# First rounds' modulation as a TensorE product in four column groups, with four load buffers

## The chip, the cores and the metric

One core of a Trainium2 chip runs the program. It has a matrix engine (TensorE), a vector engine (VectorE), an engine for activations and copies (ScalarE), GpSimd, and a queue engine (SyncE, SP in the profile) that issues most loads. The metric is the device time of one execution in microseconds; lower is better.

## The reference

One block of a hybrid network on `x` (256 tokens, 2048 wide), in float32. A conditioning vector `c` gives six modulation vectors of 2048 each, the first two of which scale and shift the normed input before the wide projection `w_in`; everything after needs that projection.

```python
mod = silu(c) @ w_ada + b_ada                       # 2048 -> 6 * 2048
sh1, sc1, gt1, sh2, sc2, gt2 = split(mod, 6)
h = rms_norm(x, norm1_g) * (1.0 + sc1) + sh1
proj = h @ w_in                                     # 2048 -> 10064
o_a = rwkv7_mix(proj[:rwkv])                        # recurrent half
o_b = nsa_mix(proj[rwkv:rwkv + nsa])                # attention half
x = x + gt1 * ((sig(m1) * (o_a @ w_o_rwkv) + sig(m2) * (o_b @ w_o_nsa)) @ w_out)
h = rms_norm(x, norm2_g) * (1.0 + sc2) + sh2
x = x + gt2 * (square(relu(h @ w_up)) @ w_down)
```

## The kernel before

All activations lie transposed: `xn[:, j]` holds rows 128 j to 128 j + 127 of the normed input's 2048 features, 256 tokens wide. Matrix products are done in three passes of a shorter float format: an operand is split into a high part (`hi`, a cast on ScalarE) and a low part (`lo = raw - hi`, on VectorE), and `mm3` (L101) adds hi*hi, lo*hi and hi*lo.

**Modulation.** `mod` is 96 columns of 128 values, kept in `modc[:, e]`. Column e is a dot product of a 128x2048 block of the transposed `w_ada` with `silu(c)` spread over all partitions (`sb`): `ada_long(e)` (L165) loads one megabyte into `ap` and lets VectorE multiply and sum it in one instruction (`ada_dot`, L156). Shift columns are 0 to 15, scale columns 16 to 31. `apb` has room for four blocks; the first four loads use all four, later ones only two (`SLOTS = 2`), so the third load from there on waits until the first one's dot is done.

**Rounds.** The projection's first nine column groups need all 2048 features, but start before all of `mod` is there: `rounds = [(0, 2), (2, 2), (4, 4), (8, 4), (12, 4)]` (L182) names the feature columns j of each round and their number. Each round first turns its columns into `am = (1 + sc) * norm1_g` and `hhi`, `hlo` (`modulate`, L326), and then runs nine groups of columns over its k rows, two at a time. One such **step** is a load `wr` of two k rows x 512 columns (352 in the first group, in three DMAs), the cast `whi`, the low part `wlo`, and 24 (18) matmuls of 256 tokens. Round 0 and round 1 have 9 steps each, round 2 and round 3 have 18 each: steps 1 to 9, 10 to 18, 19 to 36 and 37 to 54. After round 0 (which ScalarE copies) the sums of a group in PSUM (`pp`) are added to SBUF on VectorE, two banks a group (`acc_evac`); two groups, `pvp`, stay in PSUM through all rounds. `whi` and `wlo` have three buffers each, `wr` has four.

`next_ada` (L236) is called once a step and puts the loads and dots of the next round's columns among the steps: four columns for each two k rows.

**What sets the order.** The tile framework orders the instructions of each engine when the program is built, by priorities (`prio(STREAM)` comes before the main work) and its own notion of time. On the chip each engine then works through its list in order; a load waits in SP's list until its buffer is free. The names in the rows are those of the code: `ap` blocks of `w_ada`, `wr` blocks of `w_in`, `hf` an intermediate of `modulate`, `prk`, `pq`, `pl` the sums in SBUF, `pss` the sum of squares for the norm, `cps` the spread of `c`. Rows with a number behind the name tell buffers of one name apart.

Of the kernel before, what the change touches and what calls it, by code (L numbers as in the profile page):

```python
# [25 lines left out]
P_BADA, P_N1, P_N2, P_MU, P_A0, P_KK, P_KA, P_RK, P_LNW, P_LNB = 0, 96, 112, 128, 155, 163, 171, 179, 187, 195  # L26
P_QG, P_KG0, P_KG1, P_KG2, P_PEK, P_PEV, NPRM = 203, 204, 205, 206, 207, 223, 239

# [4 lines left out]
def block_kernel(ctx, tc, a):  # L33
# [128 lines left out]
    apn = [0]  # L162
    SLOTS = 2

    def ada_long(e):  # L165

        n = apn[0] if apn[0] < 4 else apn[0] % SLOTS
        r = apb[n // 2][:, n % 2]
        apn[0] += 1
        nc.sync.dma_start(r, a["w_ada_t"][e * 128:(e + 1) * 128])  # L170
        ada_dot(r, sb, prm[:, P_BADA + e:P_BADA + e + 1], modc[:, e:e + 1])
# [10 lines left out]
    rounds = [(0, 2), (2, 2), (4, 4), (8, 4), (12, 4)]  # L182
    for j in range(rounds[0][1]):
        ada_long(j)
        ada_long(16 + j)

# [56 lines left out]
    def proj(segs_of, W, ms, rhi, rlo, kps, evac, banks=None, first=True, last=True):  # L243
# [4 lines left out]
        for i, kp in enumerate(kps):  # L248
            hi, lo = weights(segs_of(kp), W)
            next_ada(ada_long if starting[0] else ada)  # L250
            todo = [[(k, m) for m in range(len(ms))] for k in range(2)]
# [39 lines left out]
    for k in range(2):  # L291
        mm(pss, ones, sqs[:, k], k == 0, k == 1)

# [7 lines left out]
    def rsqrt(out, x, scale, ep, tmp):  # L301

        e0 = {0.0: 0, 1e-6: 1, 64e-5: 2}[ep]
        act(out, x, AF.Ln, scale=scale, bias=eps[0:x.shape[0], e0:e0 + 1])
        i = act(out, out, AF.Exp, scale=-0.5)
        tt(tmp, out, out, OP.mult)
        stt(tmp, x, ep / scale, tmp, OP.add, OP.mult)
        stt(tmp, tmp, -0.5 * scale, out, OP.mult, OP.mult)
        stt(out, out, 1.5, tmp, OP.mult, OP.add)
        return i  # L310

    rs = T2("rs", [128, T])
    with tc.issue_after(log_exp([lastt])):
        rsqrt(rs, pss, 1.0 / D, 1e-6, T2("rst", [128, T]))

# [34 lines left out]
    pl = cst.tile([128, 3, T], FT, name="pl")  # L350
    pvp = [PX("pvp") for _ in range(4)]
    M4 = [(i * 128, 128) for i in range(4)]
# [19 lines left out]
    for i in range(2):  # L372
        groups.append(([(2048 + i * 512, 512)], 512, M4, None, pvp[2 * i:2 * i + 2]))
    for i in range(2):
# [9 lines left out]
    for r, (j0, n) in enumerate(rounds):  # L384
        first, last = r == 0, r == len(rounds) - 1
        with prio(START + (1 << 18)):
            stt(am[:, j0:j0 + n], modc[:, 16 + j0:16 + j0 + n], 1.0, prm[:, P_N1 + j0:P_N1 + j0 + n], OP.add, OP.mult)
            lasth = modulate(j0, n, xn)
            if first:
                hold.extend([lasth] * 0 + [None])  # L390
        if not last:
            later.extend(e for j in range(j0 + n, sum(rounds[r + 1])) for e in (j, 16 + j))
            pace[:] = [len(later) / (len(groups) * n // 2 - 1), 0]
        for cols, W, ms, dst, banks in groups:
            g = proj(wseg(cols), W, ms, hhi, hlo, range(j0 // 2, (j0 + n) // 2),
# [739 lines left out]
    with tc.issue_after(le):  # L1135
        i = rsqrt(rs2, ps[:, 0:T], 1.0 / D, 1e-6, T2("rst2", [128, T]))
    ahold[:0] = [i, i]
# [115 lines left out]
def _pack(inp):  # L1253
# [21 lines left out]
    out = {  # L1275
        "xT": g["x"].T, "c": g["c"], "w_ada_t": g["w_ada"].T, "w_in": g["w_in"], "params": p, "consts": c,
        "onehot": onehot, "w2a": np.concatenate([g["rwkv_w2"], g["rwkv_w0"][None]]), "a2": g["rwkv_a2"],
# [22 lines left out]
```

## Time and profile before

| | |
|---|---|
| median of three runs | 1647.45 us (1645.04 to 1648.28) |
| profiled execution | 1648.3 us, of which the span is 1646.5 us |
| TensorE (PE) busy | 1564.2 us, 95% |
| VectorE (DVE) busy | 1149.4 us, 70% |
| ScalarE (ACT) busy | 756.3 us, 46% |
| DMA, mean | 232 GB/s over the span, 371 GB/s in its first fortieth |

The span is what the trace shows between the first and the last instruction. Shares over the whole span hide the stretch that the change is about, the first 206 us; the tables by stage and the engines' timelines of that stretch are what to read.

### The profile page before, as it was taken

Reading aid. Unit: us, or ns where it says so; the run is one execution under the profiler, and the core shown is the slowest. Engines: PE = TensorE matmul, PEld = TensorE weight load, DVE = VectorE, ACT = ScalarE, POOL = GpSimd, SP = SyncE. Lnnn points to the kernel's source line nnn. Section 1 sums busy time; section 2 is a strip of 40 time slices with the busy share of each in tenths; the row PEclk is TensorE's granted clock in tenths of the full one; section 3 lists DMA queues with packets and bytes.
Section 4 is the critical chain, followed back from the end, with each engine's and each line's share of the span. In section 5 each row is a group of like instructions: output and inputs, shape, how many; then the busy total and the mean of one; then the engine's idle time right before and its main releaser. Section 6 shows DMA issues by size and latency. Waiting matters only on the chain.

```text
span 1646.5 us, 28130 instructions
## 1 busy us (share of the span) xinstructions
PE 1564.2 (95%) x11291; PEld 1380.2 (84%) x11291; DVE 1149.4 (70%) x1695; ACT 756.3 (46%) x1112; POOL 34.9 (2%) x60
## 2 busy tenths in 40 slices
PE   5969999999999889999999899999999999999998
PEld 4968998878889879777899788888888888888886
DVE  7999876977788766777876776666655555555555
ACT  4423358526423365656534444444444544444442
POOL 0000000000000000000000000000000000000001
PEclk9989999998999999999999999999999999999999
DMA  9999767673988777655687477878776555555564
GB/s 371 319 325 342 247 183 236 215 200 120 324 245 276 251 262 258 237 180 167 212 287 269 153 242 239 264 244 260 242 217 189 204 194 193 192 192 194 194 194 148
DMA packets 171174, 381.99 MB, mean 232 GB/s; under 512 B 29249, under 2 KB 43905, under 8 KB 166690
## 3 DMA queue, kind: packets, MB, share of 16 engines
q1 hardware_dynamic: 149344, 355.79, 65.6%
q0 software_dynamic: 4176, 14.17, 2.4%
q10 hardware_dynamic: 17523, 10.24, 2.2%
q8 instruction: 88, 1.44, 0.3%
q14 instruction: 43, 0.35, 0.1%
HBM read 370.13 MB, written 10.01 MB: 231 GB/s over the span
## 4 chain that ended last, share of the span: by engine, by line
PE 48%; DMA 4%; DVE 3%; issue 1%; ACT 1%; DVEq 0%; ACTq 0%
PE pu L99 21%; PE da L99 10%; PE db L99 10%; PE pp L99 5%; DMA ar<-in_w_ada_t 2%; DMA wr<-in_w_out 1%; DVE wlo L90 1%; PE po L99 1%; PE sps L99 1%; DMA gate<-sma 0%; ACT whi L193 0%; PE ptp L1012 0%; DVE ar L158 0%; DVE o L90 0%; ACT p L87 0%
## 5 line engine op out<-in xcount | busy, mean ns | idle before, releaser
L193 ACT CAST whi<-wr 128x1024 fp32r<-128x1024 f32 (+1 forms) x352 | 367.0, 1043 | 513.4 <-PE pp L99 125.6
L90 DVE TENSOR_TENSOR wlo<-wr,whi 128x1024 fp32r<-128x1024 f32 (+1 forms) x352 | 425.8, 1213 | 171.8 <-ACT whi L193 168.7
L99 PE MATMUL pp<-hhi,whi 128*128 128x256 f32 (+1 forms) x1072 | 309.9, 293 | 25.1 <-ACT hhi L87 22.5
L99 PE MATMUL pp<-hlo,whi 128*128 128x256 f32 (+1 forms) x1072 | 307.4, 289 | 0.2 <-DVE hlo L93 0.2
L99 PE MATMUL pp<-hhi,wlo 128*128 128x256 f32 (+1 forms) x1072 | 301.2, 290 | 6.6 <-DVE wlo L90 6.6
L90 DVE TENSOR_TENSOR wdl<-wd,wdh 128x1024 fp32r<-128x1024 f32 x128 | 156.6, 1225 | 170.9 <-ACT wdh L193 170.9
L99 PEld LDWEIGHTS pp<-hhi,whi 128*128 128x128 f32 (+1 forms) x1072 | 209.9, 197 | 33.8 <-ACT hhi L87 23.4
L193 ACT CAST wdh<-wd 128x1024 fp32r<-128x1024 f32 x128 | 134.9, 1055 | 193.7 <-PE db L99 188.6
L99 PEld LDWEIGHTS pp<-hhi,wlo 128*128 128x128 f32 (+1 forms) x1072 | 205.5, 196 | 13.0 <-DVE wlo L90 8.5
L99 PEld LDWEIGHTS pp<-hlo,whi 128*128 128x128 f32 (+1 forms) x1072 | 210.5, 196 | 5.0 <-issue 3.7
L99 PE MATMUL pu<-h2a,whi 128*128 128x512 f32 x512 | 177.2, 398 | 3.1 <-DVE h2a L93 3.1
L99 PE MATMUL pu<-h2b,whi 128*128 128x512 f32 x512 | 179.1, 397 | 0.8 <-DVE h2b L93 0.8
L99 PE MATMUL pu<-h2b,wlo 128*128 128x256 f32 x512 | 140.9, 280 | 0.0
L99 PE MATMUL pu<-h2a,wlo 128*128 128x256 f32 x512 | 135.9, 281 | 0.0
L158 DVE CUSTOM_DVE_ANT_0 ar<-ar,sb,prm 128x1024 f32<-128x1024 f32 x64 | 82.1, 1282 | 73.0 <-DMA ar<-in_w_ada_t 72.9
L99 PEld LDWEIGHTS pu<-h2b,whi 128*128 128x128 f32 x512 | 95.8, 188 | 23.9 <-DVE h2b L93 1.2
L99 PEld LDWEIGHTS pu<-h2a,whi 128*128 128x128 f32 x512 | 95.2, 189 | 24.4 <-DVE h2a L93 3.4
L99 PEld LDWEIGHTS pu<-h2a,wlo 128*128 128x128 f32 x512 | 95.5, 190 | 2.2
L158 DVE CUSTOM_DVE_ANT_0 ar<-ar,sb,adap 128x1024 f32<-128x1024 f32 x64 | 82.0, 1281 | 21.2 <-DMA ar<-in_w_ada_t 20.9
L99 PEld LDWEIGHTS pu<-h2b,wlo 128*128 128x128 f32 x512 | 95.9, 189 | 0.5
L99 PE MATMUL db<-wdh,ul 128*128 128x512 f32 x256 | 79.6, 389 | 0.0
L99 PE MATMUL db<-wdl,uh 128*128 128x512 f32 x256 | 79.6, 389 | 0.0
(342 smaller groups left out, 2676.6 us busy)
## 6 DMA issues: line engine op xcount, KB each, us to landing
wr<-in_w_in SPq DMA_DIRECT2D x136, 512.0 KB, 5.1
ar<-in_w_ada_t SPq DMA_DIRECT2D x128, 512.0 KB, 4.8
wr<-in_w_up SPq DMA_DIRECT2D x128, 512.0 KB, 4.3
wd<-in_w_down SPq DMA_DIRECT2D x128, 512.0 KB, 4.3
ap<-in_w_ada_t SPq DMA_DIRECT2D x32, 1024.0 KB, 6.6
wr<-in_w_out SPq DMA_DIRECT2D x32, 512.0 KB, 5.4
wr<-in_w_in SPq DMA_DIRECT2D x40, 256.0 KB, 3.4
wr<-in_w_o_rwkv SPq DMA_DIRECT2D x16, 512.0 KB, 4.9
```

The lines of the kernel that those rows point to most:

```text
L90: return V.tensor_tensor(out, x, y, op=op).ins
L99: return PE.matmul(out, l, r, start=start, stop=stop, skip_group_check=True).ins
L158: V.tensor_tensor_reduce(out=r, in0=r, in1=s, scale=0.5, scalar=start, op0=OP.mult, op1=OP.add, accum_out=out)
L193: S.copy(hi, raw)
```

## The change

- The columns of rounds 0 and 1 (0 to 3 and 16 to 19) are no longer dots on VectorE. `ada_pair((j, q))` handles two shift and two scale columns in four quarters q: it loads one megabyte of `w_ada_p` (a copy of `w_ada` rearranged on the host: per partition four blocks of 512 values, 256 shift and 256 scale columns each) and issues four float32 matmuls with 32 columns of weights each, `scz[:, 4q + i]` (2 silu(c) in column 0, zeros beside it), on the four column groups of the array, into the 32 rows of `adp` that belong to each. After the fourth quarter the bank is copied to `row`, and four matmuls against a column of ones add the four groups and turn the result, into `adc`; two additions put it into `modc`.
- Round 0's four quarters are issued at the start, the last two behind the norm's sum of squares; round 1's four are put into round 0.
- `later` of round 0 holds these four quarters and columns 4, 20 and 5 of round 2 (as dots); round 1 gets the other five. So round 2's eight columns are split three and five where round 1 had all eight.
- `ada_long` rotates through four buffers at all times.
- In round 0 the two `pvp` groups come last, and their four banks are allocated then.
- Two constraints (`ahold`, `hold`) put the first casts behind the norm's exponential and the first low parts behind the norm and `hlo`.

```diff
-    SLOTS = 2
...
-        n = apn[0] if apn[0] < 4 else apn[0] % SLOTS
+        n = apn[0] % 4
...
-    for j in range(rounds[0][1]):
-        ada_long(j)
-        ada_long(16 + j)
+    scz = T2("scz", [128, 16, 32])
+    V.memset(scz, 0.0)
+    sct = T2("sct", [128, 16])
+    act(sct, prm[:, P_C:P_C + 16], AF.Tanh, scale=0.5)
+    stt(scz[:, :, 0], sct, 1.0, prm[:, P_C:P_C + 16], OP.add, OP.mult)
+    adp = [None]
+
+    def ada_pair(x, after=None, copy_after=None):
+        j, q = x
+        n = apn[0] % 4
+        r = apb[n // 2][:, n % 2]
+        apn[0] += 1
+        nc.sync.dma_start(r, a["w_ada_p"][j * 256 + q * 128:j * 256 + q * 128 + 128])
+        if q == 0:
+            adp[0] = PX("adp")
+        with tc.issue_after(after) if after else contextlib.nullcontext():
+            for i in range(4):
+                mm(adp[0][32 * i:32 * i + 32], scz[:, 4 * q + i], r[:, i * 512:i * 512 + 512], q == 0, q == 3)
+        if q == 3:
+            row, ps = T2("adr", [128, 512]), PX("adc")
+            with tc.issue_after(copy_after) if copy_after else contextlib.nullcontext():
+                S.copy(row, adp[0])
+            for i in range(4):
+                mm(ps[:, i:i + 1], row[:, i * 128:i * 128 + 128], one, i == 0, i == 3)
+            for i, e in enumerate((j, 16 + j)):
+                stt(modc[:, e:e + 2], ps[:, 2 * i:2 * i + 2], 0.5, prm[:, P_BADA + e:P_BADA + e + 2], OP.mult, OP.add)
+
+    for q in range(2):
+        ada_pair((0, q))
...
+    ahold.extend([firsts[0]] * 3)
+    for q in range(2, 4):
+        ada_pair((0, q), i, firsts[0])
...
-                hold.extend([lasth] * 0 + [None])
+                hold.extend([lasth, lasth, firsts[1]])
...
+        if first:
+            later[:] = [(2, q) for q in range(4)] + [4, 20, 5]
+            pace[:] = [0.9, 0]
+        elif r == 1:
+            later[:] = [e for e in later if e not in (4, 20, 5)]
+            pace[:] = [len(later) / 8, 0]
+
-        for cols, W, ms, dst, banks in groups:
+        for cols, W, ms, dst, banks in sorted(groups, key=lambda g: g[3] is None) if first else groups:
+            if banks is not None:
+                if first:
+                    pvp.extend(PX("pvp") for _ in range(2))
+                banks = pvp[2 * banks:2 * banks + 2]
```

What the framework makes of it shows in three places. On TensorE, from the last spread of `c` to the first projection matmul, before:

```order
L99 MATMUL cps_123<-crow_94,one1_96 128x512
L99 MATMUL cps_127<-crow_94,one1_96 128x512
L99 MATMUL cps_131<-crow_94,one1_96 128x512
L99 MATMUL pss_149<-sqs_150,cs_103 128x256 x2
L99 MATMUL pp_202<-hhi_184,whi_208 128x256
```

and after:

```order
L99 MATMUL cps_131<-crow_94,one1_96 128x512
L99 MATMUL adp_143<-ap0_135,scz_137 32x512 x4
L319 MATMUL pss_157<-sqs_158,cs_103 128x256 x2
L99 MATMUL adp_143<-ap0_135,scz_137 32x512 x4
L99 MATMUL adp_143<-ap1_136,scz_137 32x512 x8
L99 MATMUL adc_203<-cs_103,adr_202 128x1 x4
L99 MATMUL pp_225<-hhi_211,whi_231 128x256
```

The sixteen small matmuls of round 0's columns stand around `pss`, and the four that turn them stand right ahead of round 0. On SP, from the load of the fourth block of `w_in`, before:

```order
L226 DMA wr_302<-in_w_in 128x2x512
L170 DMA ap0_135<-in_w_ada_t 128x2048 x2
L226 DMA wr_334<-in_w_in 128x2x512
L226 DMA wr_366<-in_w_in 128x2x512
L226 DMA wr_402<-in_w_in 128x2x512
L170 DMA ap0_135<-in_w_ada_t 128x2048 x2
L226 DMA wr_436<-in_w_in 128x2x512
```

and after:

```order
L253 DMA wr_336<-in_w_in 128x2x512
L196 DMA ap0_135<-in_w_ada_p 128x2048 x2
L196 DMA ap1_136<-in_w_ada_p 128x2048 x2
L253 DMA wr_375<-in_w_in 128x2x512
L253 DMA wr_423<-in_w_in 128x2x512
L253 DMA wr_459<-in_w_in 128x2x512
L169 DMA ap0_135<-in_w_ada_t 128x2048
L253 DMA wr_495<-in_w_in 128x2x512
```

Four megabytes stand ahead of the fifth block (`wr_334`, now `wr_375`) where two stood. On VectorE in round 1, from the additions before the low part of its third step (`wlo_585`) to that of its sixth, before:

```order
L90 TENSOR_TENSOR prk_186<-prk_186,pp_544 128x512
L90 TENSOR_TENSOR wlo_585<-wr_582,whi_584 128x1024
L90 TENSOR_TENSOR prk_186<-prk_186,pp_545 128x512
L90 TENSOR_TENSOR wlo_619<-wr_616,whi_618 128x1024
L90 TENSOR_TENSOR wlo_651<-wr_648,whi_650 128x1024
L90 TENSOR_TENSOR prk_186<-prk_186,pp_580 128x512
L158 ISA ap0_135,modc_111<-ap0_135,sb_93,prm_105 128x2048
L158 ISA modc_111 128x1
L90 TENSOR_TENSOR prk_186<-prk_186,pp_581 128x512
L90 TENSOR_TENSOR wlo_685<-wr_682,whi_684 128x1024
```

and after, from the low part of round 1's third step (`wlo_638`) to that of its fourth (the line L158 is a dot, in two instructions):

```order
L90 TENSOR_TENSOR wlo_638<-wr_635,whi_637 128x1024
L90 TENSOR_TENSOR prk_213<-prk_213,pp_597 128x512
L158 ISA ap0_135,modc_111<-ap0_135,sb_93,prm_105 128x2048
L158 ISA modc_111 128x1
L90 TENSOR_TENSOR prk_213<-prk_213,pp_598 128x512
L90 TENSOR_TENSOR prk_213<-prk_213,pp_633 128x512
L90 TENSOR_TENSOR prk_213<-prk_213,pp_634 128x512
L158 ISA ap1_136,modc_111<-ap1_136,sb_93,prm_105 128x2048
L158 ISA modc_111 128x1
L90 TENSOR_TENSOR wlo_670<-wr_667,whi_669 128x1024
```

Dots and additions have moved ahead of the low part of the fourth step. Further on in the new list, 24 dots stand between round 0's `hlo` and the low part of step 29, and none between that and the end of round 4; in the old list 18 dots stand up to the same low part, and ten behind it. From the end of round 3 to about 350 us the lists of all engines are the same but for numbers; in the middle stage they differ in places.

## Rows read from the trace of the kernel before

**Rows 1.** Stages: length, busy us by engine, clock, DMA share, GB/s

```profile
0.00:4.00 4.00, 1.05 (x2) 0.56 (x3) 0.60 (x6) 1.28 (x1) 0.20 (x4) 1.00 0.39 111
...
27.90:55.40 27.50, 27.33 (x210) 27.04 (x211) 23.07 (x26) 15.18 (x24) 0.00 (x0) 1.00 0.97 348
...
55.40:81.70 26.30, 25.54 (x212) 25.23 (x211) 25.07 (x29) 9.58 (x11) 0.00 (x0) 1.00 0.95 321
...
81.70:95.40 13.70, 0.34 (x4) 0.14 (x2) 12.02 (x15) 1.64 (x3) 0.00 (x0) 0.70 0.91 321
...
95.40:151.60 56.20, 53.66 (x419) 52.93 (x420) 53.46 (x64) 20.15 (x24) 0.00 (x0) 0.95 0.93 335
...
151.60:206.00 54.40, 52.20 (x423) 51.94 (x422) 46.68 (x55) 19.84 (x22) 0.00 (x0) 0.97 0.80 266
...
350.00:944.00 594.00, 561.03 (x5294) 502.45 (x5292) 439.08 (x840) 287.61 (x499) 24.03 (x42) 0.97 0.71 232
```

**Rows 2.** TensorE's waits, 27 to 206 us: total, times, longest

```profile
PE pp L99 <- ACT hhi L87: 22.5, 2, 13.4
PE pp L99 <- DVE wlo L90: 4.5, 4, 2.2
```

**Rows 3.** Timeline of the start: start, us, engine, line, operation, idle before

```profile
13.66 2.35 DVE L158 CUSTOM_DVE_ANT_0 ap<-ap,sb,prm 128x2048 f32<-128x2048 f32 x1
...
21.20 0.78 ACT L193 CAST whi<-wr 128x704 fp32r<-128x704 f32 x1 [1.44 <-DMA wr<-in_w_in]
...
21.87 2.34 DVE L158 CUSTOM_DVE_ANT_0 ap<-ap,sb,prm 128x2048 f32<-128x2048 f32 x1
...
26.82 0.87 DVE L93 SCALAR_TENSOR_TENSOR hf<-xn,am,rs 128x256 f32<-128x256 f32 x2
...
27.89 1.22 PE L99 MATMUL pp<-hhi,whi 128*128 128x256 f32 x4 [9.15 <-ACT hhi L87]
```

**Rows 4.** VectorE timeline, several instructions of a kind in some rows

```profile
29.54 2.34 DVE L158 CUSTOM_DVE_ANT_0 ap<-ap,sb,prm 128x2048 f32<-128x2048 f32 x1
...
31.81 2.34 DVE L158 CUSTOM_DVE_ANT_0 ap<-ap,sb,prm 128x2048 f32<-128x2048 f32 x1
...
94.29 1.67 DVE L93 SCALAR_TENSOR_TENSOR hf<-xn,am,rs 128x256 f32<-128x256 f32 x4
...
109.95 1.27 DVE L90 TENSOR_TENSOR prk<-prk,pp 128x512 f32<-128x512 f32 x2
...
122.57 2.35 DVE L90 TENSOR_TENSOR wlo<-wr,whi 128x1024 fp32r<-128x1024 f32 x2
```

**Rows 5.** TensorE timeline where 32-column weights stand; last row from 651 us

```profile
281.62 1.04 PE L99 MATMUL kss<-ksq,cs 128*32 128x512 f32 x2
...
287.81 0.28 PE L99 MATMUL pp<-hhi,wlo 128*128 128x256 f32 x1
...
288.02 1.05 PE L99 MATMUL kss<-ksq,cs 128*32 128x512 f32 x4
...
289.01 0.38 PE L99 MATMUL pp<-hhi,whi 128*128 128x256 f32 x1
...
289.23 0.28 PE L99 MATMUL pp<-hlo,whi 128*128 128x256 f32 x1
...
651.27 3.66 PE L99 MATMUL scp<-kcb,qn 128*128 128x32 f32 x32
```

**Rows 6.** DMA from 4 to 40 us; then round 0's `ap` loads

```profile
DMA packets 6131, 14.57 MB, mean 405 GB/s; under 512 B 1098, under 2 KB 3210, under 8 KB 5106
L170 SPq DMA_DIRECT2D ap<-in_w_ada_t x4: 328/344/431, 5.3 to 8.8; - x4
DMA to landing us min/median/max: 7.5/8.8/11.3
```

**Rows 7.** SP's waits up to 200 us: total, times, longest

```profile
SPq L170 <- DVE modc L158: 57.2, 24, 5.3
```

**Rows 8.** Stages, the microseconds after the hole, columns as above

```profile
96.00:100.00 4.00, 4.00 (x20) 3.89 (x20) 3.81 (x6) 0.52 (x2) 0.00 (x0) 0.50 0.69 266
```

More of the change, by code (lines that the diff above doesn't have):

```diff
@@ L26 @@
 P_BADA, P_N1, P_N2, P_MU, P_A0, P_KK, P_KA, P_RK, P_LNW, P_LNB = 0, 96, 112, 128, 155, 163, 171, 179, 187, 195
-P_QG, P_KG0, P_KG1, P_KG2, P_PEK, P_PEV, NPRM = 203, 204, 205, 206, 207, 223, 239
+P_QG, P_KG0, P_KG1, P_KG2, P_PEK, P_PEV, P_C, NPRM = 203, 204, 205, 206, 207, 223, 239, 255
 C_ID, C_MSK, C_HS, C_ONE, C_BLK, C_CUM, C_SEL, NCST = 0, 128, 192, 224, 225, 353, 609, 737
@@ L249, in proj @@
             hi, lo = weights(segs_of(kp), W)
-            next_ada(ada_long if starting[0] else ada)
+            next_ada((ada_pair if later and isinstance(later[0], tuple) else ada_long) if starting[0] else ada)
             todo = [[(k, m) for m in range(len(ms))] for k in range(2)]
@@ L291, in block_kernel @@
     for k in range(2):
-        mm(pss, ones, sqs[:, k], k == 0, k == 1)
+        i = PE.matmul(pss, ones, sqs[:, k], start=k == 0, stop=k == 1, skip_group_check=True).ins
     def log_exp(behind):
@@ L308, in rsqrt @@
         stt(tmp, tmp, -0.5 * scale, out, OP.mult, OP.mult)
-        stt(out, out, 1.5, tmp, OP.mult, OP.add)
-        return i
+        return i, stt(out, out, 1.5, tmp, OP.mult, OP.add)
     rs = T2("rs", [128, T])
     with tc.issue_after(log_exp([lastt])):
-        rsqrt(rs, pss, 1.0 / D, 1e-6, T2("rst", [128, T]))
+        firsts = rsqrt(rs, pss, 1.0 / D, 1e-6, T2("rst", [128, T]))
+    ahold.extend([firsts[0]] * 3)
+    for q in range(2, 4):
+        ada_pair((0, q), i, firsts[0])
     hhi = B16("hhi", [128, KC, T], FR)
@@ L350, in block_kernel @@
     pl = cst.tile([128, 3, T], FT, name="pl")
-    pvp = [PX("pvp") for _ in range(4)]
+    pvp = []
     M4 = [(i * 128, 128) for i in range(4)]
@@ L372, in block_kernel @@
     for i in range(2):
-        groups.append(([(2048 + i * 512, 512)], 512, M4, None, pvp[2 * i:2 * i + 2]))
+        groups.append(([(2048 + i * 512, 512)], 512, M4, None, i))
     for i in range(2):
@@ L1135, in block_kernel @@
     with tc.issue_after(le):
-        i = rsqrt(rs2, ps[:, 0:T], 1.0 / D, 1e-6, T2("rst2", [128, T]))
+        i = rsqrt(rs2, ps[:, 0:T], 1.0 / D, 1e-6, T2("rst2", [128, T]))[0]
     ahold[:0] = [i, i]
@@ L1266, in _pack @@
     p[64:96, P_MU + 26] = g["rwkv_mu"][3328:]
+    cols(P_C, g["c"])
     for at, k in ((P_A0, "rwkv_a0"), (P_KK, "rwkv_k_k"), (P_KA, "rwkv_k_a"), (P_LNW, "rwkv_ln_w"), (P_LNB, "rwkv_ln_b")):
@@ L1275, in _pack @@
     out = {
-        "xT": g["x"].T, "c": g["c"], "w_ada_t": g["w_ada"].T, "w_in": g["w_in"], "params": p, "consts": c,
+        "xT": g["x"].T, "c": g["c"], "w_ada_t": g["w_ada"].T,
+        "w_ada_p": np.concatenate([np.concatenate([g["w_ada"][:, e:e + 256] for e in (j * 128, D + j * 128)], 1)
+                                   .reshape(4, 4, 128, 512).transpose(0, 2, 1, 3).reshape(512, D) for j in (0, 2)]),
+        "w_in": g["w_in"], "params": p, "consts": c,
         "onehot": onehot, "w2a": np.concatenate([g["rwkv_w2"], g["rwkv_w0"][None]]), "a2": g["rwkv_a2"],
```

## The prediction

> **What bounds the kernel now.** I read the table by stage first [rows 1]. One "step" below is one block of `w_in` (two k rows, 512 columns, or 352 in the first group): a load, a cast `whi` on ScalarE, a low part `wlo` on VectorE, and 24 (or 18) matmuls. A round of two k rows is nine steps, 210 matmuls. TensorE begins round 0 at 27.89 us. It is busy in almost all of rounds 0 and 1 (27.9 to 55.4 and 55.4 to 81.7), does nothing for 13.7 us, and then works through rounds 2 and 3 with 2 to 3 us idle in each. In the hole VectorE is busy 12.0 of 13.7 us. The waits of TensorE say the same: 22.5 us for `hhi`, in two waits (the start and the hole), and only 4.5 us for `wlo` [rows 2]. So up to the end of round 3, at 206.0 us, there are two limits: TensorE, whose matmuls of 256 columns go 0.12 us apart (0.12 x 210 = 25.2 us a round), and VectorE, whose queue holds the low parts, the 2.3 us dots of the modulation and the additions of partial sums. From 206 us on the change alters no dot and no load; what it gains or loses before 206 us is handed through to the end.
>
> **The start.** Before, VectorE does the four dots of round 0 from 13.66 to 24.2 us, `hf` follows at 26.82, and TensorE starts at 27.89 [rows 3]. After, the same four megabytes are loaded at the same places; the last is issued at 8.8 us and lands 11.3 us later, at 20.1 [rows 6]. What a packed group of four costs must be bounded. Two matmuls of this form (32 columns of weights, 512 moving, float32) on two column groups took 1.05 us together, as one alone took 1.04 [rows 5]; one after the other they would take twice that. I take 1.05 for four as well, since the two overlapped fully, and add the wider spacing at both edges (0.21 and 0.22 in place of 0.12): 1.18 us when it stands in the main stream. The other end is four in turn, 4 x 0.85 = 3.4 us (rival 3).
>
> The Trainium skill ("TensorE: Matmul & The Clock Gate", section "Measured speedup vs the span model") gives 2.38 times for three column groups; estimated for four at that efficiency, a group would cost about 0.3 us more, 1.3 us in round 0. No run here has four yet.
>
> So the last group ends at 21.1 us. ScalarE's order has the cast of the first `whi` ahead of the copy of the sums, and it waits for its load until 21.20 [rows 3]: cast (0.78 for 704 elements) to 21.9, copy (512, so 0.6) to 22.5. The four turning matmuls have 128 columns of weights and one moving; nearest are 16 of 32 columns in 3.66 us [rows 5], so 0.9: 23.4. Two additions and `am`, 0.3; from `hf` to the first matmul 1.07 as before (26.82 to 27.89). The start is 24.9, a gain of 3.0 us. If the groups run at the low clock it is up to 1 us less. The two low parts that stood ahead of `hf` and `hlo` now come behind them; that is in the sum, since nothing stands between `am` and `hf`. Making `scz` (a clearing, a tanh, a product of 16 columns) costs nothing: VectorE waits for its first inputs then, and ScalarE's tanh stands under the loads that end at 20.1.
>
> **Round 0 in the new order.** It also holds the four groups for round 1 and their turning: 4 x 1.18 + 0.9 = 5.6 us of TensorE, added to the 25.2. Nothing hides them: TensorE is the busy engine there. That the `pvp` groups come last in round 0 moves matmuls, and adds none. What they take away is four dots of 2.27 us (29.54 to 31.81 [rows 4]) from VectorE. But the order of the loads puts four megabytes ahead of the fifth block, where two stood before. Counting bytes: the inputs and constants 2.6 MB, eight ada loads 8.4, five blocks 2.5 make 13.4 MB; the queues moved 0.4 MB by 4 us and then 405 GB/s [rows 1, 6], so the fifth block lands at 36.0. VectorE has then been idle since 30.8, and its low part starts at 37.1: 6.3 us of wait. It waits 2.3 us more for the seventh cast, whose buffer TensorE frees only after step 4 (at 24.9 + 10.8 + 4.7 = 40.4), and about 3 us in shorter waits. Sum 11.6 us, which TensorE does not see at once.
>
> **VectorE's queue, the main term.** The four load buffers let four ada loads be out at a time. SP before waited 57.2 us for `modc`, in 24 waits [rows 7]: that was the brake on the dots. With it gone, the order has the dots packed ahead of the low parts: in round 1 four additions and three dots stand between the low parts of the 3rd and 4th step, where one addition stood before. By the 29th step's low part (the 11th of round 2's 18) all 24 remaining dots are done; before, by the same step, only 18 of 28 since 29.54 us. A dot done early makes TensorE wait for the low part behind it.
>
> I price both queues with the same spacings [rows 4]: low part 1.14 (0.80 for 704 elements, by size), dot 2.27, addition of a bank 0.60 and of the small one 0.33 (by size), `hf` and `hlo` 0.40 each.
> - Before, from 29.54 to the 29th low part: 26 low parts 28.6, 18 dots 40.9, 16 + 2 + 2 additions 11.5, modulation of two rounds 5.0: 86.0 us. The row at 122.57 says that it ended at 124.9, 95.4 us later; so 9.4 us were waits. The method holds.
> - After, from 24.9 + 1.65 = 26.5: 28 low parts 30.9, 24 dots 54.5, additions 11.5, modulation of three rounds 8.6: 105.5 us. With no wait at all it ends at 132.0; with the 11.6 above at 143.6. A lower bound of the waits: the ninth cast needs TensorE through step 6 (24.9 + 16.6 + 5.6 = 47.1, and 1.05 for the cast), while VectorE's work up to there ends at 45.6; so 2.6, and 134.6.
>
> Behind the 29th step no dot is left until round 4 is over, and VectorE's load in round 3 (two thirds of TensorE's) hides everything: TensorE runs on at 0.12 us. Steps 29 to 54 are 612 matmuls, 73.4 us, less 0.5 that are done before the low part: 143.6 + 72.9 = 216.5 us for the end of round 3, against 206.0 before. Before, the same 612 took 81.1 us from 124.9, 8.2 more than at full speed: this is what is gained back. **Net: 10.5 us later.** By its own parts: start -3.0, groups +5.6, and 34.8 us of TensorE's waits in place of the 13.7 us hole and 13.2 us of smaller losses before (206.0 - 27.9 less six times 25.2).
>
> **Bounds.** With the least waits the end is 207.5 (+1.5). Above, the clock: after the hole the matmuls ran at a granted 0.50 for four microseconds, the 1.2 GHz level [rows 8]. Waits of several microseconds stand in rounds 1 and 2 after the change; four microseconds at half the clock cost two, and I allow that twice where TensorE is next to limit: +14.5. The Trainium skill (same page, section "HAM oscillation — how this bites in real kernels") describes idle stretches between bursts that throttle each burst again; by it the higher end is the likelier one; the row at 96 us agrees for one long stretch, and no row here shows it for several short ones. After 350 us the order of the middle stage also shifts in places. TensorE is idle there 594 - 561 = 33 us [rows 1]; an estimate of a tenth of that, 4 us either way, goes into the range.
>
> The profiled execution took 1648.3 us, 1.8 outside its span of 1646.5, and 0.85 above the median. 1648.3 + 10.5 - 0.8 = 1658.0.
>
> **Rivals.**
> 1. *The hole simply closes.* If the dots found room in the idle time of VectorE, the start gives 3.0, the hole 13.4, and the groups take 5.6: 10.8 us faster, 1637. For it: VectorE has four dots fewer, and was busy only 23.1 of 27.5 us in round 0 [rows 1]. Against: its queue is in order, and 105.5 us of work before the 29th low part leave no room. It decides if that low part ends before 125 us. Chance 0.09.
> 2. *Within noise.* VectorE waits little in round 0 (the fifth block lands by 31, not 36, and the ninth cast comes on time): +1.5 and the middle stage either way, 1645 to 1651. Chance 0.14.
> 3. *The column groups do not overlap.* Then each of the eight groups costs 3.4 us warm: 4 x 2.35 = 9.4 us more in round 0 and, since they then follow each other slower than the loads land, 5 or more at the start: 1672 or above. The pair in [rows 5] speaks against it. Chance 0.05. This is also the case in which the change does not do what it says.
> 4. The forecast, slower by way of VectorE's order: 0.72.
>
> **How the numbers follow.** About 0.2%, 3.3 us, is what a measurement here can tell from no change. The forecast's own range is 1.5 - 4 to 14.5 + 4 us, with its low part counted to "same": 1645 to 1666. To keep no more than 2 in 10 outside, the range ends at 1669, some way to rival 3, and leaves rival 1 out. Faster 0.10 (rival 1 and a lucky middle), same 0.14, slower 0.76.
>
> **What would show it.** Right: the first `pp` matmul near 25 us; four `adp` matmuls within about 1.1 us; the fifth block's cast near 36; in round 1 waits of TensorE for `wlo` of several microseconds instead of one for `hhi`; the 29th low part near 140 or later; round 3 without a wait, ended near 216. Wrong: a 29th low part before 130 us, dots that wait for their loads rather than low parts that wait for dots, or a middle stage that moves by more than 5 us by itself.

## The result

The changed kernel took 1669.04 us in the median of four runs (1663.39 to 1672.62), the kernel before 1646.55 beside it: 1.0133 times as long, 95% interval 1.0102 to 1.0164. That is 22.5 us slower. The profiled execution of the changed kernel took 1669.56 us with a span of 1667.8, 21.3 us longer than the span of before. The direction and the mechanism were forecast; the size was forecast as 10.5 us.

The changed kernel by stage (columns as in [rows 1]): its rounds 0, 1, 2 and 3, then the stretch from 210 matmuls into the last round (25.2 us behind the end of round 3 where nothing stops TensorE) to the first product of the MLP, called *the middle* below, then the rest. TensorE's next 114 matmuls of the last round lie in the middle; they take 13.9 us in both kernels.

```profile
27.00:63.30 36.30, 33.47 (x250) 29.36 (x251) 23.84 (x28) 17.06 (x26) 0.00 (x0) 0.92 1.03 407
63.30:105.20 41.90, 30.54 (x211) 29.57 (x211) 40.19 (x48) 10.63 (x13) 0.00 (x0) 0.81 0.96 353
105.20:170.50 65.30, 56.08 (x423) 54.79 (x421) 60.13 (x74) 21.56 (x26) 0.00 (x0) 0.92 0.82 274
170.50:220.90 50.40, 50.40 (x423) 50.40 (x422) 30.47 (x33) 18.32 (x18) 0.00 (x0) 1.00 0.64 182
246.00:948.10 702.10, 661.07 (x6207) 593.10 (x6205) 519.55 (x959) 347.78 (x616) 28.56 (x50) 0.97 0.71 227
948.10:1667.80 719.70, 711.34 (x3605) 604.43 (x3605) 429.63 (x488) 312.80 (x372) 6.16 (x6) 0.99 0.65 211
```

The same middle in the kernel before:

```profile
231.10:926.20 695.10, 658.77 (x6208) 589.55 (x6206) 518.72 (x959) 347.68 (x616) 28.52 (x50) 0.98 0.71 229
```

Against [rows 1]: round 0 is 36.3 us long where it was 27.5. Round 1 is 41.9 where it and the hole behind it were 40.0. Round 2 is 65.3 where it was 56.2, and in it VectorE is busy 60 of 65 us. Round 3 is 50.4 us of nothing but matmuls where it was 54.4. The end of round 3 comes at 220.86 in place of 205.95, **14.9 us later**, and the matmul at 281.62 us comes still 14.9 later, at 296.54. The middle, with the same matmuls, is **7.0 us** longer: 4.7 us of it are idle time of TensorE, 2.3 are matmuls that run slower. The rest gives back 0.7. Sum 21.2.

TensorE's waits from 24 to 235 us in the changed kernel (total, times, longest), to be held against [rows 2]:

```profile
PE pvp L99 <- DVE wlo L90: 10.1, 3, 6.0
PE pp L99 <- DVE wlo L90: 7.1, 4, 2.9
PE pp L99 <- DVE pl L90: 3.2, 1, 3.2
PE pp L99 <- DVE prk L90: 2.5, 1, 2.5
PE adc L99 <- ACT adr L205: 1.6, 1, 1.6
PE pp L99 <- ACT hhi L87: 1.6, 1, 1.6
```

The hole for `hhi` is gone. In its place TensorE waits 17.2 us for low parts and 5.7 us for additions (`pl`, `prk`) that free its PSUM banks. The longest wait, and what VectorE does meanwhile (VectorE's timeline of the changed kernel, columns as in [rows 3]):

```profile
71.68 1.88 DVE L90 TENSOR_TENSOR prk<-prk,pp 128x512 f32<-128x512 f32 x3
73.47 2.35 DVE L158 CUSTOM_DVE_ANT_0 ap<-ap,sb,prm 128x2048 f32<-128x2048 f32 x1
...
75.74 2.35 DVE L158 CUSTOM_DVE_ANT_0 ap<-ap,sb,prm 128x2048 f32<-128x2048 f32 x1
...
78.02 1.22 DVE L90 TENSOR_TENSOR wlo<-wr,whi 128x1024 fp32r<-128x1024 f32 x1
```

TensorE's timeline at that place:

```profile
73.04 0.28 PE L99 MATMUL pvp<-hlo,whi 128*128 128x256 f32 x1
79.29 0.58 PE L99 MATMUL pvp<-hhi,wlo 128*128 128x256 f32 x1 [5.97 <-DVE wlo L90]
```

ScalarE had done the cast for that low part long before:

```profile
69.75 1.05 ACT L220 CAST whi<-wr 128x1024 fp32r<-128x1024 f32 x1 [4.37 <-DMA wr<-in_w_in]
```

Two dots for round 2, 4.5 us, stand ahead of a low part that TensorE needs at 73. VectorE waits for nothing here: the dots had their data, the low part had its cast at 70.8, and only the order of the queue put the dots first.

### The profile page after: what moved, and what is told of

The parts are those of the page before. It is cut to its first block, busy times and chain, and to the rows that moved or that the text cites. A ratio compares the mean times of both kernels' runs of the same rounds, so it can differ in the third digit from the quotient of the medians.

```text
span 1667.8 us, 28298 instructions
## 1 busy us (share of the span) xinstructions
PE 1583.7 (95%) x11371; PEld 1392.5 (83%) x11371; DVE 1135.2 (68%) x1685; ACT 758.4 (45%) x1115; POOL 34.9 (2%) x60
## 4 chain that ended last, share of the span: by engine, by line
PE 72%; DVE 12%; DMA 10%; ACT 3%; issue 3%; ACTq 1%; DVEq 0%; SPq 0%
PE pu L99 21%; PE pp L99 21%; PE da L99 10%; PE db L99 10%; DVE wlo L90 4%; DMA wr<-in_w_in 3%; DMA ar<-in_w_ada_t 3%; DVE ap L158 2%; PE pvp L99 2%; DMA wr<-in_w_out 2%; ACT whi L220 1%; DVE ar L158 1%; PE po L99 1%; PE sps L99 1%; PE xps L99 1%
## 5 line engine op out<-in xcount | busy, mean ns | idle before, releaser
L99 PE MATMUL pp<-hhi,wlo 128*128 128x256 f32 (+1 forms) x1072 | 304.5, 292 | 10.5 <-DVE wlo L90 10.4
L99 PEld LDWEIGHTS pp<-hhi,whi 128*128 128x128 f32 (+1 forms) x1072 | 211.2, 197 | 20.8 <-issue 14.3
L158 DVE CUSTOM_DVE_ANT_0 ar<-ar,sb,prm 128x1024 f32<-128x1024 f32 x64 | 82.1, 1282 | 68.9 <-DMA ar<-in_w_ada_t 68.8
L99 PEld LDWEIGHTS pu<-h2b,whi 128*128 128x128 f32 x512 | 95.7, 188 | 23.4 <-DVE h2b L93 1.0
L158 DVE CUSTOM_DVE_ANT_0 ar<-ar,sb,adap 128x1024 f32<-128x1024 f32 x64 | 82.0, 1281 | 23.2 <-DMA ar<-in_w_ada_t 20.6
```

The costliest lines, as they stand in the source:

```text
L99: return PE.matmul(out, l, r, start=start, stop=stop, skip_group_check=True).ins
L158: V.tensor_tensor_reduce(out=r, in0=r, in1=s, scale=0.5, scalar=start, op0=OP.mult, op1=OP.add, accum_out=out)
```

## The experiments

Three theories. **Theory 1** (the prediction's): four load buffers let the dots be placed bunched on VectorE's queue, ahead of low parts and additions. **Theory 2**: the cost is the product on TensorE and what its loads push back. **Theory 3**: part of the loss is the middle, whose static order comes out differently with every change ahead of it, and has nothing to do with the change's content.

All twelve, with the kernel before and the changed one. "Rounds" is the end of round 3 (in brackets by how much the start of the middle moved, where that is another amount), "middle" its length. "Low clock" is a sum over sixty equal slices of the middle, each slice's length times one minus its granted clock; "idle" is the middle less TensorE's busy time. These four are us of one profiled execution. "Time" is the difference between the medians of the kernel and of the kernel before beside it, "ratio" that of the runs, with its 95% interval.

| kernel | rounds | middle | low clock | idle | time | ratio |
|---|---|---|---|---|---|---|
| before | 205.95 | 695.1 | 17.2 | 36.3 | 0 | 1 |
| changed | 220.86 | 702.1 | 23.8 | 41.0 | +22.5 | 1.0133 [1.0102, 1.0164] |
| buffers_alone | 219.85 | 707.0 | 29.3 | 36.0 | +25.4 | 1.0155 [1.0117, 1.0193] |
| two_buffers | 201.10 | 717.8 | 35.7 | 46.4 | +20.3 | 1.0119 [1.0070, 1.0168] |
| held | 202.21 (+0.65) | 698.1 | 24.0 | 40.1 | +8.0 | 1.0048 [1.0026, 1.0069] |
| buffers_held | 206.89 (+3.80) | 713.7 | 28.9 | 51.2 | +20.8 | 1.0129 [1.0101, 1.0157] |
| one_group | 226.68 | 712.3 | 35.7 | 39.2 | +35.3 | 1.0218 [1.0180, 1.0257] |
| before_pace60 | 205.38 | 705.3 | 27.2 | 39.7 | +13.7 | 1.0082 [1.0053, 1.0111] |
| before_pace70 | 207.11 | 697.3 | 25.6 | 32.5 | +1.6 | 1.0010 [0.9991, 1.0029] |
| two_pace60 | 200.95 | 717.6 | 34.4 | 49.4 | +18.6 | 1.0117 [1.0087, 1.0147] |
| two_pace70 | 200.18 | 699.0 | 27.4 | 35.7 | -0.8 | 1.0001 [0.9983, 1.0019] |
| two_pace75 | 200.90 | 697.0 | 30.8 | 33.3 | +1.2 | 1.0017 [0.9999, 1.0034] |
| late_two70 | 205.49 | 698.7 | 27.3 | 37.1 | 0.0 | 1.0006 [0.9980, 1.0032] |
| late_two65 | 205.90 | 700.1 | 22.9 | 41.9 | +12.9 | 1.0075 [1.0049, 1.0101] |

A profiled execution can lie some us from the median of its kernel: late_two65's took 1653.72 us, its median is 1662.52; two_pace75's 1644.43, its median 1647.79. If the whole difference sits in the middle (an estimate), their usual middles are 9 and 3 us longer than the table says. The rounds vary less: the five kernels that differ from the kernel before or from two_buffers in the pace alone, so not in the order of the rounds, end them within 1.2 us of it.

### buffers_alone: the kernel before with four buffers

```diff
-        n = apn[0] if apn[0] < 4 else apn[0] % SLOTS
+        n = apn[0] % 4
```

> The kernel before with one edit: the load buffers of the dots rotate over all four, not over two after the first four. No product on TensorE, no early columns, no new waits on the startup. Theory 1 (four buffers let the dots of rounds 1 to 3 be placed bunched, two in a step, on VectorE's in-order queue, ahead of the low parts and the additions that TensorE waits for): the 29th low part ends later than the 124.9 us of the kernel before, since it then has some 10 more dots of 2.2 us ahead of it; the end of round 3 moves from 205.95 to 208 or later, and rounds 2 and 3 show waits of TensorE on low parts. Theory 2 (the cost is in the product and in the later load of the fifth block): the end of round 3 stays within 1 us of 205.95 or comes earlier. Theory 3 (a third of the cost is the middle stage, in another static order): the stretch from the end of round 3 to the first product of the MLP (720.2 us in the kernel before, 727.3 in the changed one) moves by up to 7 us in either direction, with no tie to what round 0 does.

This one line gives the whole loss: 1.0155, and rounds that end 13.9 us later, without the product and with the loads of the start as they were. All 32 dots stand ahead of the 29th low part, where 22 did, and it ends at 146.9 in place of 124.9. Its waits (24 to 235 us) have the pattern of the changed kernel:

```profile
PE pp L99 <- DVE wlo L90: 12.9, 8, 2.5
PE pp L99 <- ACT hhi L87: 9.2, 1, 9.2
PE pvp L99 <- DVE wlo L90: 5.5, 3, 3.3
PE pp L99 <- ACT whi L193: 3.2, 2, 1.6
PE pp L99 <- DVE pl L90: 1.8, 1, 1.8
```

The 9.2 us for `hhi` are the start, which before had too. The hole is gone here as well, and 18.4 us of waits for low parts stand in its place. Theory 1 holds; theory 2 is not needed for the rounds. Theory 3 had allowed 7 us for the stretch from the end of round 3 to the MLP; it is 12.0 us longer.

### two_buffers: the changed kernel with the dots on two buffers

```diff
     def ada_long(e):
-        n = apn[0] % 4
+        n = apn[0] % 2
```

> The changed kernel with one edit: the dots rotate over two of the four buffers, as they did before; the product of rounds 0 and 1 keeps its four. Theory 1: the dots spread out to one in two steps, the 29th low part has fewer dots ahead of it, and the end of round 3 falls from 220.86 us to between 205 and 212; the time falls by 9 us or more if the middle stage is what it is in the changed kernel. Theory 2: the end of round 3 stays at 219 to 222 us. Theory 3: the stretch from the end of round 3 to the first product of the MLP differs from 727.3 us by several us, whatever round 3 does.

The rounds end at 201.10, which is 19.8 us ahead of the changed kernel, 4 us better than expected, and **4.9 us ahead of the kernel before**. This is what the rest of the change (the product, with the order that goes with it) is worth in the rounds when the dots are not bunched. Its waits, and its hole behind round 1 (13.7 us long in [rows 1]):

```profile
PE pp L99 <- ACT hhi L87: 9.2, 2, 7.5
PE pp L99 <- DVE wlo L90: 1.9, 3, 0.7
```

```profile
60.10:86.40 26.30, 25.47 (x213) 25.27 (x211) 25.79 (x28) 8.93 (x9) 0.00 (x0) 1.00 0.97 332
86.40:94.10 7.70, 0.28 (x3) 0.07 (x1) 7.66 (x13) 1.58 (x3) 0.00 (x0) 0.79 0.92 318
```

Round 0 ends 4.7 us later than before, and the hole is 6.0 us shorter: VectorE does eight dots between the start of round 0 and the end of the hole, where it did twelve.

Yet the time is only 2 us under the changed kernel's. The middle takes it all back: 717.8 us.

### held: the changed kernel with each dot behind the low part of its step

```diff
     def ada_dot(r, s, start, out):
-        with behind():
+        with (tc.issue_after(lastlo[0]) if lastlo[0] is not None and starting[0] else behind()):
             V.tensor_tensor_reduce(out=r, in0=r, in1=s, scale=0.5, scalar=start,
...
         with behind():
-            tt(lo, raw, hi.bitcast(FT), OP.subtract)
+            lastlo[0] = tt(lo, raw, hi.bitcast(FT), OP.subtract)
...
```

> The changed kernel with one edit: every dot of the rounds may be placed on VectorE's queue only behind the low part of its own step; buffers, product and columns stay. Theory 1: the low parts come without dots in front, VectorE is ahead of TensorE again by round 1, and the end of round 3 falls from 220.86 us to 197 to 206, at or below the 205.95 of the kernel before. Theory 2: TensorE still has the product in its queue and the fifth block still lands late, so the end of round 3 stays at 216 or later. Theory 3: as for the others, the middle stage moves by several us by itself.

The four buffers stay, and the dots are not bunched: round 3 ends at 202.2, as theory 1 wants. But the first 210 matmuls of the last round give 4.4 us back (29.6 us; 25.2 before), so that behind them the kernel is 0.65 us behind the kernel before.

### buffers_held: the kernel before with four buffers and held dots

```diff
-        n = apn[0] if apn[0] < 4 else apn[0] % SLOTS
+        n = apn[0] % 4
...
-        with behind():
+        with (tc.issue_after(lastlo[0]) if lastlo[0] is not None and starting[0] else behind()):
             V.tensor_tensor_reduce(out=r, in0=r, in1=s, scale=0.5, scalar=start,
...
-            tt(lo, raw, hi.bitcast(FT), OP.subtract)
+            lastlo[0] = tt(lo, raw, hi.bitcast(FT), OP.subtract)
...
```

> The kernel before with the dots on all four buffers (alone: end of round 3 at 219.85 us) and every dot of the rounds behind the low part of its own step. Theory 1 (it is the bunched place of the dots on VectorE's queue, not the number of buffers or their loads): the end of round 3 falls back to 200 to 208 us, about the 205.95 of the kernel before. Rival: the four loads in flight take the transfers' time from w_in, whatever the order on VectorE, and it stays at 214 or more. The middle: a further draw, between 695 and 718 us.

206.9 against 219.85 with the buffers alone. With the product and without it, it is the dots' place in VectorE's order that costs, not the buffers or the loads in flight. Here too the last round loses some (2.9 us) and the middle is long (713.7), so the time is not better.

### one_group: the four matmuls of a group in one column group

```diff
-                mm(adp[0][32 * i:32 * i + 32], scz[:, 4 * q + i], r[:, i * 512:i * 512 + 512], q == 0, q == 3)
+                mm(adp[0][0:32], scz[:, 4 * q + i], r[:, i * 512:i * 512 + 512], q == 0 and i == 0, q == 3 and i == 3)
...
-                S.copy(row, adp[0])
+                S.copy(row[0:32], adp[0][0:32])
...
-                mm(ps[:, i:i + 1], row[:, i * 128:i * 128 + 128], one, i == 0, i == 3)
+                mm(ps[:, i:i + 1], row[0:32, i * 128:i * 128 + 128], one[0:32], i == 0, i == 3)
```

> The changed kernel with one edit: the four matmuls of a group all add into rows 0 to 31 of the bank, one column group, so that they cannot lie beside each other; the copy and the turning matmuls take those 32 rows. It prices the four column groups. By the changed kernel's profile four packed matmuls took 1.05 to 1.07 us, about what one takes at that clock and width, so here a group should take up to four times that, 4.2 us at full clock. Two such products of four groups each are added in the startup and round 0: plus 3 us for each of the eight groups, four of them ahead of round 0. If TensorE's own time is what the change pays for (theory 2), the end of round 3 comes 12 to 25 us after 220.86; if VectorE's queue sets it (theory 1), the groups inside round 0 lie in its waits, and only those of the startup count: 3 to 8 us.

TensorE's timeline of the changed kernel: the fourth quarter of the start and the first in round 0 (four matmuls have eight records).

```profile
21.29 1.07 PE L99 MATMUL adp<-ap,scz 128*32 128x512 f32 x8 [1.43 <-DMA ap<-in_w_ada_p]
...
32.37 1.06 PE L99 MATMUL adp<-ap,scz 128*32 128x512 f32 x8
...
33.37 0.39 PE L99 MATMUL pp<-hlo,whi 128*128 128x256 f32 x1
```

The same in one_group, three quarters in a row:

```profile
20.66 10.49 PE L99 MATMUL adp<-ap,scz 128*32 128x512 f32 x24
```

Three quarters take 10.49 us, 3.5 each (4.2 were expected); packed, one takes 1.07, at the same granted clock of 1.00. Four float32 matmuls in four column groups lie side by side almost fully, a factor of 3.3. Six of the eight quarters ran ahead of round 0, which began at 39.77, 12.8 us later than in the changed kernel. Of that 5.8 us are left at the end of round 3. That is within theory 1's 3 to 8 us: most of what TensorE loses early lies beside VectorE's queue.

### before_pace60, before_pace70: only the middle is perturbed

The pace of the dots in the recurrence is the one thing changed in the kernel before; the order first differs at some 420 to 430 us.

```diff
-    pace[0] = 0.65
+    pace[0] = 0.6
```

> The kernel before with one number changed, far behind the rounds: the pace of the dots in the recurrence (stage y, from 465 us) is 0.60 in place of 0.65. The first 2,631 of TensorE's 9,322 rows keep their order, up to that stage; nothing of the start is touched. Theory 3 (the middle's length hangs on which static order the scheduler happens to give, through TensorE's gaps and the low clock that follows them, and not on what the change does in the start): the end of round 3 stays within 1 us of 205.95, and the stretch from the last round (231.1) to the first product of the MLP (695.1 us long in the kernel before, 702.1 in the changed one, 707.0 with four buffers alone, 717.8 with two buffers) changes by 3 to 20 us, and the sum of span times one minus granted clock over that stretch (16.5 us before, 24 in the changed one, 36 with two buffers) changes with it. Rival: the middle lengthens because of what the changed start leaves behind (dots, buffers, transfers), then this kernel stays within 2 us of the kernel before.

> The same edit with 0.70 in place of 0.65: a second draw. Theory 3: the start as before, the middle 3 to 20 us off 695.1, by another amount than with 0.60. Rival: within 2 us of the kernel before.

With 0.60 the middle is 10.3 us longer and the kernel 1.0082 times as long. On every engine the order is the same up to the recurrence; there, on VectorE, it first differs in this (the order as built; - before, + before_pace60):

```
 L90 TENSOR_TENSOR wlo_4739<-wr_4736,whi_4738 128x1024
-L158 ISA ar_4743,adap_4742<-ar_4743,sb_93,prm_105 128x1024
-L158 ISA adap_4742 128x1
-L158 ISA ar_4746,modc_111<-ar_4746,sb_93,adap_4742 128x1024
-L158 ISA modc_111 128x1
-L90 TENSOR_TENSOR wlo_4795<-wr_4792,whi_4794 128x1024
+L90 TENSOR_TENSOR wlo_4788<-wr_4785,whi_4787 128x1024
+L158 ISA ar_4792,adap_4791<-ar_4792,sb_93,prm_105 128x1024
+L158 ISA adap_4791 128x1
```

The two half-column dots move behind one more low part, and everything behind them is laid out anew. So a middle that is 7 us longer needs no cause in the start. With 0.70 it is 2.2 us longer and the time cannot be told from the kernel before, which goes with the rival; one draw hit and one did not.

The middle in before_pace60:

```profile
230.50:935.90 705.40, 665.66 (x6208) 596.04 (x6206) 519.13 (x959) 347.98 (x616) 28.58 (x50) 0.96 0.70 225
```

The same 6,208 matmuls are busy for 665.7 us in place of 658.8, at a granted clock of 0.96 in place of 0.98.

### two_pace60, two_pace70, two_pace75: the long middle of two_buffers

The same line in two_buffers, with 0.6, 0.7 and 0.75.

```diff
-    pace[0] = 0.65
+    pace[0] = 0.7
```

> The changed kernel with the dots on two buffers (whose start is 4.9 us ahead of the kernel before at the end of the rounds, and whose middle is 22.7 us longer), and the pace of the dots in the recurrence 0.60 in place of 0.65. Theory 3: the end of round 3 stays within 1 us of 201.1, and the middle falls from 717.8 to between 693 and 712, since the draw of two_buffers was the worst of six; the time is 1640 to 1660 us. Rival: the changed start makes the middle long, and it stays at 714 or more.

> As the last, with 0.70. Theory 3: the start at 201.1, the middle 693 to 712, the time 1640 to 1660 us. Rival: the middle stays at 714 or more.

> The changed kernel with the dots on two buffers and the pace in the recurrence 0.75 in place of 0.65: a last draw of the middle, looking for a kernel that beats both. Theory 1 puts the end of round 3 at 200 to 201.2 us, 5 to 6 us ahead of the kernel before, whatever the pace. Theory 3 puts the middle anywhere from 695 (the shortest of twelve so far) to 718 us, so the time between 1641 and 1664 us; it beats the kernel before only with a middle under about 700.

0.60 leaves the middle at 717.6, outside what theory 3 gave and as its rival had it. 0.70 and 0.75 bring it to 699.0 and 697.0 with the same start, so the start does not make it long. The time falls by some 20 us from one number that acts behind 416 us. Neither beats the kernel before: 1.0001 and 1.0017, both intervals with 1 in them, though their rounds end 5 to 6 us sooner. For two_pace75 the condition that was named, a middle under about 700, was met and did not suffice: in the two profiled executions its stages add up to 3.9 us less than those of the kernel before, and the medians do not bear that out. The kernel before has the shortest middle of all fourteen.

The middle of two_buffers and of two_pace70:

```profile
226.30:944.10 717.80, 671.39 (x6207) 601.74 (x6206) 521.50 (x959) 349.72 (x616) 28.64 (x50) 0.95 0.69 222
```

```profile
225.30:924.40 699.10, 663.40 (x6208) 595.19 (x6206) 517.95 (x959) 349.10 (x616) 28.77 (x50) 0.96 0.71 227
```

How such a place looks in two_buffers: four stretches of four us from 568.

```profile
568.00:572.00 4.00, 0.00 (x0) 0.00 (x0) 3.27 (x5) 0.00 (x0) 0.00 (x0) 1.00 0.22 32
572.00:576.00 4.00, 2.97 (x14) 2.97 (x15) 3.95 (x6) 1.65 (x4) 0.00 (x0) 0.51 0.70 230
576.00:580.00 4.00, 3.48 (x10) 1.72 (x9) 3.86 (x8) 2.19 (x5) 1.08 (x2) 0.50 0.81 230
580.00:584.00 4.00, 4.00 (x14) 2.99 (x14) 1.45 (x3) 0.03 (x1) 0.00 (x0) 0.50 0.48 181
```

What TensorE waits for there (562 to 592 us), and what VectorE does:

```profile
PE pp L99 <- DVE wlo L90: 5.3, 1, 5.3
```

```profile
568.70 1.28 DVE L158 CUSTOM_DVE_ANT_0 ar<-ar,sb,adap 128x1024 f32<-128x1024 f32 x1 [4.07 <-DMA ar<-in_w_ada_t]
...
571.76 1.22 DVE L90 TENSOR_TENSOR wlo<-wr,whi 128x1024 fp32r<-128x1024 f32 x1
```

A half-column dot stands at the head of VectorE's queue and waits 4.07 us for its load; the low part is behind it; TensorE stops for 5.3 us; then it works at a granted 0.50, the 1.2 GHz level, from 573 to at least 584. It is the same kind of fault as in the rounds, side work ahead of urgent work in an in-order queue (there the dots had their data, here one waits for it), and it is paid twice: once as a wait and once as clock.

### late_two70, late_two65: two quarters behind later blocks of w_in

The dots on two buffers and the pace 0.70 (0.65 in late_two65), and:

```diff
-        nc.sync.dma_start(r, a["w_ada_p"][j * 256 + q * 128:j * 256 + q * 128 + 128])
+        with tc.issue_after(lastw[0]) if j and q > 1 else contextlib.nullcontext():
+            nc.sync.dma_start(r, a["w_ada_p"][j * 256 + q * 128:j * 256 + q * 128 + 128])
...
-            later[:] = [(2, q) for q in range(4)] + [4, 20, 5]
-            pace[:] = [0.9, 0]
+            later[:] = [(2, q) for q in range(4)]
+            pace[:] = [0.5, 0]
...
-            later[:] = [e for e in later if e not in (4, 20, 5)]
```

> The changed kernel with three edits: the dots on two buffers, the pace in the recurrence 0.70 (together the kernel with the start at 200.2 us and 1647.1 us in all), and the third and fourth quarter of the second product loaded behind the sixth and seventh block of w_in, not ahead of the fifth. It tells what the late fifth block costs. If the 8.5 us for which VectorE stands still ahead of the fifth block's low part (42.7 us) set the end of round 0, that low part starts 4 to 5 us earlier, at 37 to 39, round 0 ends at 55 to 57 in place of 59.5, and the end of round 3 comes at 195 to 198. Rival: the next hole takes it back; the end of round 1 waits for the dots of columns 4 to 7 anyway (7.7 us at 86 us with two buffers), the end of round 3 stays at 199.5 to 201 and only the hole at 86 us grows. Theory 3 on the middle, for both: between 695 and 718 us, another draw. Time 1638 to 1665 us.

> The same with the pace in the recurrence left at 0.65: the start as in the last, a further draw of the middle, between 695 and 718 us.

The edit is wider than "three edits": round 0's list loses columns 4, 20 and 5 and its pace goes from 0.9 to 0.5. The fifth block's low part starts at 36.67 in place of 42.09 in two_pace70, as expected, and round 0 ends at 59.9 all the same (59.5 there). Its load was issued at the same time in both (24.05 and 24.27); what moved is the place of its cast on ScalarE's list, at 35.60 between two copies in place of 41.01 behind them. Neither theory had the end of round 3: at 205.5 the gain of 5 us is gone. Round 0 of late_two70:

```profile
26.50:59.90 33.40, 33.40 (x249) 29.45 (x250) 18.87 (x23) 16.82 (x26) 0.00 (x0) 0.91 0.98 376
```

TensorE is busy in all of it. With the dots on two buffers the end of round 0 is TensorE's own work, and the late cast of the fifth block is free. Most of the lost 5 us are in round 2, which holds 12 dots where two_pace70 has 10; the cause was not traced further.

## Why the prediction was right, and where its size was off

- **The direction and the main term hold.** "A dot done early makes TensorE wait for the low part behind it": buffers_alone shows it by itself (+13.9 us at the end of round 3), two_buffers, held and buffers_held take it away by two different means. The size does not: 22.5 us against 10.5. The 1669.04 stands at the very end of the stated range, beyond the 1666 to which the forecast's own terms reach. The rest was room towards rival 3, which did not happen, so that the range reaches this far is luck.
- **The brake.** "With it gone" is not what the trace shows. SP waits for `modc` up to 200 us nearly as long in the changed kernel (first row) as in two_buffers (second row); before it was 57.2 us in 24 waits:

```profile
SPq L169 <- DVE modc L158: 44.7, 19, 3.6
SPq L169 <- DVE modc L158: 46.2, 19, 4.4
```

  What differs is the order that was built. Ahead of the 29th low part stand 24 of 24 dots in the changed kernel and 32 of 32 in buffers_alone, but 14 of 24 in two_buffers, 12 of 24 in held, 20 of 32 in buffers_held and 22 of 32 before.
- **The start** was to gain 3.0 us and gained 0.9. The cast of the first `whi`, put at 21.20 as before, waited for its load to 22.62 (the last quarter, too, came at 21.29 and not at 20.1); the turning matmuls took 1.49, not 0.9. Together 2.0. From `hf` (25.92) to the first matmul were 1.08 us, as said. ScalarE's timeline of the changed kernel:

```profile
22.62 0.78 ACT L220 CAST whi<-wr 128x704 fp32r<-128x704 f32 x1 [3.91 <-DMA wr<-in_w_in]
23.31 0.58 ACT L205 COPY adr<-adp 128x512 f32<-128x512 f32 x1
```

- **The packed groups** took the predicted 1.05 to 1.07 us, but for the very first (1.94 us, at 13.87). Round 0 is 36.3 us less a stall of 3.1 at 57.7, so 33.2: the 27.5 of before and the 5.6 that were forecast. The Trainium skill ("TensorE: Matmul & The Clock Gate", section "Measured speedup vs the span model"), by the estimate weighed there, would have added 0.3 us a group (four times that is 1.2, not 1.3); the four groups in round 0 show none of it. Rival 3 falls, and one_group gives its price (a median of 1682.22 us, where 1672 or above was said).
- **VectorE's queue.** The 29th low part was to end at 143.6 and ended at 147.9:

```profile
42.14 2.36 DVE L90 TENSOR_TENSOR wlo<-wr,whi 128x1024 fp32r<-128x1024 f32 x2 [7.82 <-ACT whi L220]
...
146.68 1.23 DVE L90 TENSOR_TENSOR wlo<-wr,whi 128x1024 fp32r<-128x1024 f32 x1
```

  It began 2.1 us later (27.0 + 1.65) and held 147.9 - 28.65 = 119.2 us: the 105.5 of work, and 13.8 of waits where 11.6 were summed. The later start (2.1) and the further waits (2.2) account for the 4.3 us. The longest wait, for the fifth block, was 7.8 us, not 6.3, and not for the reason given: its load, issued at 24.35 and 11.2 us under way by the median of the three loads there, landed near 35.5, as forecast, but the cast came at 41.06 and not near 36. On ScalarE's list it stood behind copies of round 0's sums that waited 3.94 us for TensorE:

```profile
34.62 1.30 ACT L388 COPY prk<-pp 128x512 f32<-128x512 f32 x2 [1.28 <-PE pp L99]
39.86 1.30 ACT L388 COPY prk<-pp 128x512 f32<-128x512 f32 x2 [3.94 <-PE pp L99]
41.06 2.00 ACT L220 CAST whi<-wr 128x1024 fp32r<-128x1024 f32 x2
```

- **The end of round 3** was to be 72.9 us behind that low part and was 73.0, round 3 without a wait, as forecast. So its 220.9 in place of 216.5 is only the error above.
- **The middle** is the term that was mis-sized: an estimate of 4 us either way around zero, from a tenth of its idle time, and it was +7.0 in the profile. So what stood at 206 us was not just "handed through to the end": 14.9 became 21.2. "A middle stage that moves by more than 5 us by itself" was named as what would make the forecast wrong, and that sign came. The profiles put it between 2 and 23 us longer in thirteen programs and never shorter. An estimate centred on zero was the wrong one here: the kernel before turned out to have the shortest middle of all. That a new order alone makes a middle this long is shown in before_pace60; that it made the changed kernel's own 7.0 us is inferred, since the changed kernel was run with one pace only.
- **The clock** was allowed 4 us in the rounds. The stretches are there (0.81 granted in round 1, 0.92 in round 2). By the stages' rows, the rounds of the changed kernel hold 23.4 us in which TensorE is idle, and its matmuls take 13.7 us more than 0.12 us apiece and 5.6 for the groups (before: 19.0 and 7.9). So the 14.9 us are -0.9 for the start, +5.6 for the groups, +4.4 idle and +5.8 slower running; the forecast called the last two together waits. This adds up and does not say what caused what: where VectorE's queue ends last, a slower matmul only takes the place of a wait, and from the 29th low part on the sum came out with no clock term. In the middle low clock goes from 17 to 36 us over the fourteen programs, and the middle rises with it loosely (two_pace75 has 30.8 us of it and the second shortest middle); it rises with idle time as much. The Trainium skill ("TensorE: Matmul & The Clock Gate", section "HAM oscillation — how this bites in real kernels") describes stops that throttle the matmuls behind them, and the rows of two_buffers at 568 us agree: a stop of 5.3 us, then the lower level. How much of the middle each of idle and clock causes was not separated.
- **Rival 1** (the hole closes into a gain) had the right sign for the product alone: with two buffers its rounds end 4.9 us sooner, not 10.8, because a hole of 7.7 us stays. It was lost to the order that came with the buffers, and not to the groups.
- **Columns 4, 20 and 5**, which the change puts on round 0's list, do nothing: built with round 2's eight columns all on round 1's list, the program has the same instructions in the same order on every engine. The split into three and five is in the code only; this variant was not run.

## What to carry to other kernels

More load buffers are not free when an in-order queue is shared: a shortage of buffers can be what makes the scheduler place side work behind the work that another engine waits for. When a buffer is added, look first at what then moves ahead of what in the built order, and either keep the shortage or tie the side work behind the urgent instruction. And before a difference of some ten us is put down to an edit, perturb a number that the edit does not touch: where a scheduler lays out the rest of the kernel, that alone moved this one by 13.7 us, and the stretch that the edit is about has to be read by itself.

## What the runs showed of the hardware

- Four float32 matmuls of 32 weight columns and 512 moving ones, in four column groups, took 1.07 us together and 3.5 us in one group.
- A stop of TensorE of 5.3 us (ended at 573.0 in two_buffers) was followed by at least eleven us at a granted 0.50 (to 584); at half the clock they cost about five, an estimate, as much as the stop.
- Executions of one kernel differ by up to 14 us here (1639.63 to 1653.74 in 13 runs of the kernel before), so that a gain of 5 us in the rounds has to be read in its own stage.
